# Making the low parts of all projection weight tiles on VectorE instead of GpSimd in a two-layer hybrid decoder trunk

## Chip, cores and metric

The kernel runs on one core of one Trainium2 chip. The metric is the time of one execution in microseconds (us), as the median of several runs. One more execution was taken with the hardware profiler on; all rows in this document come from such profiled executions.

## What is computed

The reference applies two layers to a residual stream x of 1024 tokens by 1024 channels, all in float32:

```python
for l in range(DEPTH):                       # DEPTH = 2
    h = x @ w_in                             # 1024 x 2912
    o_sb = stick_breaking_attention(...)     # 4 heads of 64
    o_mla = mla_mixer(...)                   # 4 heads, softmax attention with low-rank q and kv
    o_rwkv = rwkv7_mixer(...)                # 8 heads, a recurrence over tokens
    mix = concatenate([o_sb, o_mla, o_rwkv], axis=-1) @ w_o
    x = layer_norm(DEEPNORM_ALPHA * x + mix, ln1_g, ln1_b)
    u_act, u_gate = split(x @ ffn_w_up, 2)   # d_ff = 2816
    hid = gelu(causal_depthwise_conv(u_act)) * u_gate
    x = layer_norm(DEEPNORM_ALPHA * x + hid @ ffn_w_down, ln2_g, ln2_b)
```

## The kernel before

Most large products are made of three matrix products. Each float32 operand is split into a high part, a copy in TensorE's reduced type fp32r, and a low part, the operand minus its high part. TensorE then adds high times high, high times low and low times high in PSUM (`mm3`, L203 to L205). The split is one helper, `split`: ScalarE always makes the high part (L198), and the low part is one subtraction (L199) on VectorE, or on GpSimd where the caller names it:

```python
def split(self, hi, lo, src, eng=None):
    self.nc.scalar.copy(hi, src)                                                          # L198
    (eng or self.nc.vector).tensor_tensor(lo, src, hi.bitcast(F32), op=ALU.subtract)      # L199
```

Both inputs of the subtraction and its output lie in SBUF. A weight tile is 128 partitions by 1024 columns. `wload` (L230) loads one from HBM into `raw` and splits it into `whi` and `wlo`; each of the three names has two buffers, so the high part of a tile waits until TensorE has used the tile before last.

A layer runs in four stages. **Phase A** (`phase_a`, about 37 to 540 us of the span in layer 0) makes the input projections and the RWKV work. A loop over four feature tiles `ft` (L1100) makes the k, r and v projections of each by `proj_rw`, prepares them (`rw_prep`, `rw_stage1`), and after each pair starts the inversion of small triangular blocks (`rw_inv`), a generator whose many VectorE steps (L720 to L762) are threaded between other work. After it comes the chain over tokens (`rw_chain`), and beside it the projections for stick-breaking attention (`proj_sb`). **Attention** (about 540 to 735 us) interleaves both attentions; at its end the first two tiles of the output weight are split (L1202). The **output projection** (`oproj`) splits the other six tiles (L949), multiplies, normalizes and transposes. The **FFN** (`ffn`, about 760 to 1550 us) is the rest. Layer 1 follows the same pattern from about 1560 us on.

The splits that name GpSimd are: nine per layer in phase A, for `ft` 1 to 3 (L1101); six per layer in `proj_sb` (L265, L271); two per layer at the end of attention (L1202, tile `w0l`); two per layer in `oproj`, k = 2 and 5 (L949, tile `wol`); two small ones per layer in `mla_prep` (tile `wl`). GpSimd also splits some attention operands (`lo4`, L370), masks the diagonal blocks of stick-breaking attention (L393), multiplies in `rw_stage1` (L640), and serves the chain (L879, L899).

Every engine runs its instructions in one fixed order, which the framework's scheduler writes when the program is built, from the order of the code, the offsets in the table `PRIORITY`, and its own estimate of how long each instruction takes on its engine. An instruction that waits holds everything behind it on that engine. When an instruction goes to another engine, the scheduler writes all the orders anew, so other instructions move too.

Of the kernel before, what the change touches and what calls it, by code (L numbers as in the profile page):

```python
# [17 lines left out]
P = 128  # L18
# [6 lines left out]
SBQ, SBK, SBV = 0, 256, 512  # L25
# [44 lines left out]
class Body:  # L70
# [190 lines left out]
    def proj_sb(self, l, pool, step):  # L261
        nc, W = self.nc, self.a["w_in"][l]
        for j in range(2):
            for base, dst in ((SBQ, self.sqd), (SBK, self.skd)):
                hi, lo = self.wload(W, [(base + j * P, P)], nc.gpsimd)  # L265
                d = self.t(pool, [P, S], "pst", bufs=4)
                self.proj_copy(hi, lo, d)
                nc.sync.dma_start(dst[j], d)
                step(4)
        for j in range(2):  # L270
            hi, lo = self.wload(W, [(SBV + j * P, P)], nc.gpsimd)  # L271
            d = self.t(pool, [P, S], "pst", bufs=4)
            self.proj_copy(hi, lo, d)
            o = self.t(pool, [P, S], "pst", bufs=4)
            for q in range(2):
                pt = self.ps2()
                for i in range(4):
                    ii = 4 * q + i
                    nc.tensor.transpose(pt[:, i * P : i * P + P], d[:, ii * P : ii * P + P], self.ident)
                nc.vector.tensor_copy(o[:, q * 512 : q * 512 + 512], pt)  # L280
            step(4)
            nc.sync.dma_start(self.svd[j], o.rearrange("p (i v) -> p i v", v=P))
# [652 lines left out]
    def oproj(self, l, wr, nxt, side, cm, other, xsrc, co, cx):  # L935
        nc, a = self.nc, self.a
        with cm:
            c = cm
            mp = self.pool(c, "mixp", side=side)
            tp = self.pool(c, "opt", bufs=3, side=side)  # L940
            wh = self.t(mp, [P, KT - 2, D], "woh", F32R)
            wl = self.t(mp, [P, KT - 2, D], "wol", F32R)
            wos = [(self.w0h[:, k], self.w0l[:, k]) for k in range(2)] + [(wh[:, k], wl[:, k]) for k in range(KT - 2)]
            gb = self.bcast(mp, a["ln1_g"][l], "gb")
            bb = self.bcast(mp, a["ln1_b"][l], "bb")
            for k in range(2, KT):
                if k >= len(wr):
                    wr.append(self.wo_load(l, k))
                self.split(*wos[k], wr[k], nc.gpsimd if k % 3 == 2 else None)  # L949
            co.close()  # L950
            self.new_xT(self.pool(cx, "xT", side=other))
            zs = []
            for i in reversed(range(NT)):
                s = slice(i * P, i * P + P)
                mh, ml = nxt
                z = self.t(tp, [P, D], "z")
                nc.sync.dma_start(z, xsrc[s, :])
                zs.append(z)
                ps = self.mm_ps()
                for h in range(2):  # L960
                    hs = slice(h * 512, h * 512 + 512)
                    for k in range(KT):
                        self.mm3(ps[:, hs], mh[:, k, :], ml[:, k, :], wos[k][0][:, hs], wos[k][1][:, hs], k == 0, k == KT - 1)
                    nc.vector.scalar_tensor_tensor(z[:, hs], z[:, hs], ALPHA, ps[:, hs], op0=ALU.mult, op1=ALU.add)
                if i:
                    nxt = self.mix_load(i - 1)
                self.ln_apply(z, z, gb, bb, tp)
                nc.sync.dma_start(self.x1d[s, :], z)
                if i + 1 < NT:
                    self.x_transpose(zs[-2], i + 1, "mt")  # L970
            W = a["ffn_w_up"][l]
            pre = []
            for j in range(2):
                w = self.wload(W, [(j * DFF, P)])
                ps = self.mm_ps()
                self.proj_half(ps, w, 1)
                pre.append((w, ps))
            self.x_transpose(zs[-1], 0, "mt")
        return pre
# [85 lines left out]
    def phase_a(self, l, side, other, lp, co, cc):  # L1065
        nc, a = self.nc, self.a
        c2 = ExitStack()
        ip = self.ip = self.pool(co, "rwi", side=other)
        pp = self.pp_ = self.pool(co, "pst", side=other)
        with ExitStack() as c:  # L1070
            kp = self.pool(c, "mlak", side=other)
            mw = self.pool(c, "mlaw", bufs=2, side=other)
            mc = self.proj_mla(l, pp)
            self.mla_prep(l, mc, kp, mw)
        tpa = self.tpa = self.pool(c2, "rwp", side=other)
        tp = self.pool(c2, "rws", side=other)
        self.q2n, self.q4n = 5, 2
        d = self.proj_rw(l, 12, pp, "pst")
        nc.scalar.activation(d[0:64, :], d[0:64, :], AF.Tanh)
        self.lora = [self.t(tpa, [P, S], f"lora{i}", F32R) for i in range(2)]  # L1080
        self.split(*self.lora, d)
        w2a2 = [self.t(tpa, [P, 512], f"w2a2{i}", F32R) for i in range(2)]
        raw = self.q2(tp)
        nc.sync.dma_start(raw[0:64, :], a["rwkv_w2"][l])
        nc.sync.dma_start(raw[64:128, :], a["rwkv_a2"][l])
        self.split(*w2a2, raw)
        self.Vz = []
        for b in range(1):
            z = self.t(tp, [P, S], f"Vz{b}")
            nc.gpsimd.memset(z, 0.0)  # L1090
            self.Vz.append(z)
        A6 = self.t(ip, [P, 6, NCH, C], "Aa")
        inv = None

        def step(n):
            for _ in range(n):
                if inv is not None:
                    next(inv, None)

        for ft in range(4):  # L1100
            eng = nc.gpsimd if ft else None  # L1101
            k = self.proj_rw(l, 4 + ft, pp, "pst", eng)
            step(6)
            prep = self.rw_prep(ft, k, w2a2, tp)
            r = self.proj_rw(l, ft, pp, "pst", eng)
            step(6)
            v = self.proj_rw(l, 8 + ft, pp, "pst", eng)
            step(99)
            u = (0, 2, 4, 2)[ft]
            for hf in range(2):  # L1110
                self.rw_stage1(ft, hf, [r, k, v], prep, A6[:, u : u + 2], tp)
            if ft % 2:
                inv = self.rw_inv(ft // 2, ip, A6[:, 2 * (ft // 2) : 2 * (ft // 2) + 4])
        c2.close()
        kp = self.pool(cc, "rwk", side=other)
        self.tl = self.pool(cc, "rwl", side=other)
        tp = self.pool(cc, "rwt", side=other)
        g2 = self.t(kp, [P, 512], "g2")
        nc.sync.dma_start(g2, a["rwkv_g2"][l])
        sg = self.sg = self.proj_rw(l, 13, kp, "sg")  # L1120
        nc.scalar.activation(sg, sg, AF.Sigmoid)
        self.rw_chain_state(kp)
        ch = self.rw_chain(0, g2, tp)
        for _ in ch:
            step(3)
        step(99)
        ch = self.rw_chain(1, g2, tp)

        def cstep(n):
            next(ch, None)  # L1130

        self.proj_sb(l, pp, cstep)
        for _ in ch:
            pass

    def run(self):
        nc, a, tc = self.nc, self.a, self.tc
# [27 lines left out]
        for l in range(L):  # L1165
# [15 lines left out]
            with ExitStack() as c:  # L1181
# [17 lines left out]
                nxt = self.mix_load(NT - 1)  # L1199
                wr = [self.wo_load(l, k) for k in range(6)]  # L1200
                for k in range(2):
                    self.split(self.w0h[:, k], self.w0l[:, k], wr[k], nc.gpsimd)  # L1202
            cp.close()
            with ExitStack() as c:
                self.psum(c, ps=(512, 2), mt=(512, 2))
# [42 lines left out]
```

## Time and profile before

| | |
|---|---|
| median of 3 runs | 3118.68 us (3115.67 to 3125.54) |
| the profiled execution's own time | 3115.81 us |
| its span, first to last instruction | 3114.1 us |
| TensorE (PE) busy | 2955.1 us, 95% |
| VectorE (DVE) busy | 1790.4 us, 57% |
| ScalarE (ACT) busy | 1043.3 us, 34% |
| GpSimd (POOL) busy | 328.5 us, 11% |
| mean granted TensorE clock | 0.98 |

PE stands for TensorE's matmuls, PEld for its weight loads, DVE for VectorE, ACT for ScalarE, POOL for GpSimd and SP for the queue that issues the DMAs. In a row, `out<-in` are tile names with their numbers left out, then the shape. In a timeline, `[x <-y]` means that the engine sat idle for x us before the instruction, and y was the event that ended it. The granted clock is given as a share of full speed: 1.00 is 2.4 GHz, 0.50 is 1.2 GHz.

### The profile page before, as it was taken

What the parts mean: (1) busy time and instruction counts of PE and PEld (TensorE: products, weight loads), DVE (VectorE), ACT (ScalarE), POOL (GpSimd) and SP (SyncE); (2) the same over time, 40 slices, a digit from 0 to 9 for tenths busy, and PEclk for the clock granted to TensorE, in tenths of its full rate; (3) what the DMA queues carried; (4) which work ended last, traced back from release to release, by engine and by line L of the source; (5) the groups of instructions that cost most, each with busy time, mean ns of one, the idle gap of its engine ahead of it and who ended that gap; (6) DMA issues with size and microseconds to landing.
All of it is one profiled execution on the core that took longest, in us unless ns stands there. A gap on an engine that the chain in (4) does not pass through costs nothing. (4 is left out here: it accounts for less than half of the span.)

```text
span 3114.1 us, 41891 instructions
## 1 busy us (share of the span) xinstructions
PE 2955.1 (95%) x16572; PEld 2339.9 (75%) x16572; DVE 1790.4 (57%) x2842; ACT 1043.3 (34%) x1801; POOL 328.5 (11%) x346
## 2 busy tenths in 40 slices
PE   8998999888999999999999888999899999999998
PEld 6666777666888888888876667776678888888887
DVE  4569673886644444444645687658865443444436
ACT  5443443763222112221244443447622111212120
POOL 0111231132000000000001121320410000000000
PEclk9998999999999999999999999999999999999999
DMA  4343656413421111111124446563234111111111
GB/s 131 98 143 87 197 176 194 120 52 123 168 68 55 48 41 48 55 48 55 61 81 117 119 114 196 171 203 93 86 126 162 54 41 41 48 55 48 54 48 55
DMA packets 338260, 301.78 MB, mean 97 GB/s; under 512 B 24200, under 2 KB 302992, under 8 KB 338064
## 3 DMA queue, kind: packets, MB, share of 16 engines
q1 hardware_dynamic: 338064, 299.11, 32.4%
q8 instruction: 131, 2.15, 0.3%
q14 instruction: 65, 0.53, 0.1%
HBM read 208.87 MB, written 90.18 MB: 96 GB/s over the span
## 5 line engine op out<-in xcount | busy, mean ns | idle before, releaser
L203 PE MATMUL psmm<-xTh,whi 128*128 128x512 f32 x2144 | 858.3, 400 | 0.0
L204 PE MATMUL psmm<-xTl,whi 128*128 128x512 f32 x2144 | 856.6, 400 | 0.0
L205 PE MATMUL psmm<-xTh,wlo 128*128 128x512 f32 x2144 | 854.2, 398 | 0.0
L198 ACT CAST whi<-raw 128x1024 fp32r<-128x1024 f32 x152 | 159.9, 1052 | 1108.4 <-PE psmm L204 1100.7
L203 PEld LDWEIGHTS psmm<-xTh,whi 128*128 128x128 f32 x2144 | 406.2, 189 | 94.4 <-issue 5.3
L204 PEld LDWEIGHTS psmm<-xTl,whi 128*128 128x128 f32 x2144 | 406.0, 189 | 93.5 <-issue 3.9
L205 PEld LDWEIGHTS psmm<-xTh,wlo 128*128 128x128 f32 x2144 | 405.7, 189 | 93.5 <-issue 4.4
L199 DVE TENSOR_TENSOR wlo<-raw,whi 128x1024 fp32r<-128x1024 f32 x122 | 148.9, 1220 | 430.2 <-ACT whi L198 422.6
L1050 DVE TENSOR_TENSOR y<-y,psps 128x512 f32<-128x512 f32 x288 | 196.4, 687 | 171.7 <-PE psps L205 171.4
L203 PE MATMUL psps<-wdh,hh 128*128 128x512 f32 x672 | 267.0, 397 | 0.0
L204 PE MATMUL psps<-wdl,hh 128*128 128x512 f32 x672 | 263.1, 392 | 0.0
L205 PE MATMUL psps<-wdh,hl 128*128 128x512 f32 x672 | 260.3, 392 | 0.0
L913 POOL TENSOR_TENSOR lrs<-lrs,mhalf 128x1 f32<-128x1 f32 x32 | 29.3, 914 | 1650.4 <-DVE lrs L912 1650.4
L203 PEld LDWEIGHTS psps<-wdh,hh 128*128 128x128 f32 x672 | 126.1, 188 | 36.4 <-ACT hh L198 5.5
L205 PEld LDWEIGHTS psps<-wdh,hl 128*128 128x128 f32 x672 | 126.2, 188 | 27.1
L204 PEld LDWEIGHTS psps<-wdl,hh 128*128 128x128 f32 x672 | 126.3, 188 | 25.8
L1025 DVE TENSOR_TENSOR cv<-cv,psmm 128x1024 f32<-128x1024 f32 x44 | 53.7, 1221 | 142.8 <-PE psmm L205 137.9
L199 DVE TENSOR_TENSOR wdl<-raw,wdh 128x1024 fp32r<-128x1024 f32 x42 | 51.4, 1225 | 89.0 <-ACT wdh L198 89.0
L199 POOL TENSOR_TENSOR wlo<-raw,whi 128x1024 fp32r<-128x1024 f32 x30 | 74.8, 2494 | 194.7 <-ACT whi L198 178.3
L839 PE MATMUL pspa<-RBl,PSl 128*128 128x128 f32 x512 | 71.5, 287 | 17.7 <-ACT QC L842 9.3
L1020 ACT ACTIVATE cv<-cv 128x1024 f32<-128x1024 f32 x44 | 46.7, 1061 | 115.8 <-DVE cv L1019 115.8
L839 PEld LDWEIGHTS pspa<-RBl,PSl 128*128 128x128 f32 x512 | 64.9, 197 | 25.2 <-ACT QC L842 11.2
(444 smaller groups left out, 4696.0 us busy)
## 6 DMA issues: line engine op xcount, KB each, us to landing
raw<-in_ffn_w_up_dram SPq DMA_DIRECT2D x88, 512.0 KB
raw<-in_w_in_dram SPq DMA_DIRECT2D x44, 512.0 KB
raw<-in_ffn_w_down_dram SPq DMA_DIRECT2D x44, 512.0 KB
rbd<-RB SPq DMA_DIRECT2D x64, 256.0 KB
PSl<-psd SPq DMA_DIRECT2D x32, 512.0 KB
RBl<-rbd SPq DMA_DIRECT2D x32, 512.0 KB
psd<-Vz SPq DMA_DIRECT2D x64, 128.0 KB
xxd<-X SPq DMA_DIRECT2D x64, 128.0 KB
```

The lines of the kernel that those rows point to most:

```text
L198: self.nc.scalar.copy(hi, src)
L199: (eng or self.nc.vector).tensor_tensor(lo, src, hi.bitcast(F32), op=ALU.subtract)
L203: mm(out, lh, rh, start=start, stop=False)
L204: mm(out, lh, rl, start=False, stop=False)
L205: mm(out, ll, rh, start=False, stop=stop)
L839: nc.tensor.matmul(pQ[:, f, e, :], PSh[:, f, h, e, :], RBh[:, f, h, e, :], start=True, stop=True)
L913: nc.gpsimd.tensor_tensor(rs, rs, self.mhalf[:, 0:1], op=ALU.pow)
L1020: nc.scalar.activation(cv, cv, AF.Gelu)
L1025: nc.vector.tensor_tensor(cv, cv, pg, op=ALU.mult)
L1050: nc.vector.tensor_tensor(y[:, i, hs], y[:, i, hs], ps, op=ALU.add)
```

## The change

The four places that named GpSimd for the low part of a weight tile of the input or output projection now leave the choice to `split`, which takes VectorE. The small splits of `mla_prep` and the attention operands of `lo4` stay on GpSimd. That moves 19 subtractions of 128x1024 per layer, 38 in all.

```diff
@@ proj_sb
-                hi, lo = self.wload(W, [(base + j * P, P)], nc.gpsimd)
+                hi, lo = self.wload(W, [(base + j * P, P)])
...
-            hi, lo = self.wload(W, [(SBV + j * P, P)], nc.gpsimd)
+            hi, lo = self.wload(W, [(SBV + j * P, P)])
@@ oproj
-                self.split(*wos[k], wr[k], nc.gpsimd if k % 3 == 2 else None)
+                self.split(*wos[k], wr[k])
@@ phase_a
-            eng = nc.gpsimd if ft else None
+            eng = None
@@ run
-                    self.split(self.w0h[:, k], self.w0l[:, k], wr[k], nc.gpsimd)
+                    self.split(self.w0h[:, k], self.w0l[:, k], wr[k])
```

The scheduler's new orders differ in phase A far beyond the 38 rows. Three places on VectorE, all in layer 0; each is a piece of the difference, with `-` for before and `+` for the change.

First, `rw_stage1` for `ft` = 1, around 186 to 196 us of the trace of before. `kk` and `ta` are its inputs, `q_298` and `q_299` the tiles that it hands to TensorE, `wlo_1862` and `wlo_2003` the low parts of the next two weight tiles:

```order
 L614 SCALAR_TENSOR_TENSOR kk_1435<-pst_1375,pv_66_286,kk_1435 128x1024
-L638 SCALAR_TENSOR_TENSOR q_298_1611<-kk_1435,q_296_1604 128x4x63
+L199 TENSOR_TENSOR wlo_1862<-raw_1860,whi_1861 128x1024
 L307 TENSOR_SCALAR shc_1547<-psmm_1548,pv_66_286 128x1
 L308 SCALAR_TENSOR_TENSOR pst_1546<-psmm_1548,pv_66_286,pst_1546 128x511
+L638 SCALAR_TENSOR_TENSOR q_298_1611<-kk_1435,q_296_1604 128x4x63
...
 L646 TENSOR_TENSOR ta_1434<-ta_1434,pst_1375 128x512
 L648 TENSOR_TENSOR q_299_1612<-ta_1434,q_297_1605 128x4x64 x2
-L649 SCALAR_TENSOR_TENSOR ta_1434<-pst_1482,pv_66_286,ta_1434 128x512
+L199 TENSOR_TENSOR wlo_2003<-raw_2001,whi_2002 128x1024
 L305 TENSOR_TENSOR pst_1546<-pst_1546,shc_1547 128x1
```

One low part now stands ahead of the instructions that make `q_298` and `q_299`, the other behind them.

Second, the end of that `rw_stage1` and the start of the inversion, around 219 to 239 us. `q_360` and `q_363` are the low parts of `kk` for `ft` = 2, which TensorE sums over heads (L592); `LA` is the inversion's input:

```order
+L199 TENSOR_TENSOR q_360_1984<-kk_1960,q_359_1983 128x512
+L199 TENSOR_TENSOR q_363_1992<-kk_1960,q_362_1991 128x512
 L684 TENSOR_TENSOR Aa_877<-pspa_1827,maskA_94 128x256
 L685 TENSOR_TENSOR RB_1811<-pspa_1827,maskA_94 128x4x64
 L684 TENSOR_TENSOR Aa_877<-pspy_1828,maskA_94 128x256
 L685 TENSOR_TENSOR RB_1811<-pspy_1828,maskA_94 128x4x64
-L720 STREAM_TRANSPOSE LA_1924<-Aa_877 32x1024 x2
-L305 TENSOR_TENSOR pst_1866<-pst_1866,shc_1867 128x1
-L308 SCALAR_TENSOR_TENSOR pst_1866<-psmm_1896,pv_66_286,pst_1866 128x511
-L720 STREAM_TRANSPOSE LA_1924<-Aa_877 32x1024 x2
+L720 STREAM_TRANSPOSE LA_1924<-Aa_877 32x1024 x4
```

The two low parts moved from behind the four transposes to ahead of them.

Third, the start of the chain, around 384 to 392 us. `QC_3213` is the chain's first operand, `pd` and `T` belong to the second inversion:

```order
 L724 TENSOR_TENSOR pd_3286<-LA_3284,T_3285 128x392
-L725 TENSOR_REDUCE T_3285<-pd_3286 128x2x14
-L724 TENSOR_TENSOR pd_3286<-LA_3284,T_3285 128x450
-L725 TENSOR_REDUCE T_3285<-pd_3286 128x2x15
-L724 TENSOR_TENSOR pd_3286<-LA_3284,T_3285 128x1024
 L840 TENSOR_TENSOR QC_3213<-pspa_3214,arl_3207 64x2x2x64
 L841 TENSOR_TENSOR QC_3213<-pspa_3214,ident_60 64x2x2x64
 L840 TENSOR_TENSOR QC_3213<-pspa_3222,arl_3207 64x2x2x64
 L841 TENSOR_TENSOR QC_3213<-pspa_3222,ident_60 64x2x2x64
```

Four instructions of the inversion that stood ahead of the chain's first operand now stand behind it.

## Rows read from the trace of the kernel before

**Rows 1.** The page: busy time, share of the span and instructions of each engine.

```profile
PE 2955.1 (95%) x16572; PEld 2339.9 (75%) x16572; DVE 1790.4 (57%) x2842; ACT 1043.3 (34%) x1801; POOL 328.5 (11%) x346
```

**Rows 2.** Stretches: from:to, length, busy us (instructions) by engine, granted clock, DMA.

```profile
140.00:160.00 20.00, 17.11 (x122) 12.13 (x121) 13.90 (x28) 8.13 (x19) 4.37 (x4) 1.00 0.38 106
...
140.00:380.00 240.00, 216.32 (x1548) 163.39 (x1546) 180.38 (x315) 107.86 (x209) 43.97 (x47) 0.95 0.48 134
196.00:206.50 10.50, 10.50 (x60) 7.70 (x58) 3.68 (x9) 3.99 (x13) 0.20 (x1) 0.70 0.43 112
...
220.00:300.00 80.00, 66.76 (x479) 50.44 (x477) 74.09 (x115) 32.85 (x59) 16.94 (x11) 0.91 0.34 96
380.00:540.00 160.00, 147.74 (x1333) 117.30 (x1333) 93.11 (x201) 55.83 (x110) 40.49 (x35) 0.99 0.59 186
690.00:745.00 55.00, 43.70 (x279) 31.11 (x279) 41.49 (x61) 27.68 (x66) 19.67 (x16) 0.91 0.40 122
860.00:1520.00 660.00, 660.00 (x2896) 541.99 (x2895) 279.86 (x296) 133.99 (x127) 0.00 (x0) 1.00 0.17 51
```

**Rows 3.** Waits of PE from 110 to 745 us: total us, times, longest.

```profile
PE pspq L671 <- DVE q L648: 8.0, 2, 4.3
PE pspa L336 <- DVE mexp L397: 8.0, 8, 3.0
...
PE pspq L592 <- DVE q L199: 4.8, 1, 4.8
```

**Rows 4.** Groups on L199 by shape: count, busy us, mean ns, idle before them.

```profile
L199 POOL TENSOR_TENSOR wlo<-raw,whi 128x1024 fp32r<-128x1024 f32 x30 | 74.8, 2494 | 194.7 <-ACT whi L198 178.3 <-issue 15.7 <-DMA psd<-T 0.6
...
L199 POOL TENSOR_TENSOR w0l<-raw,w0h 128x1024 fp32r<-128x1024 f32 x4 | 10.7, 2679 | 12.8 <-ACT w0h L198 12.8
L199 POOL TENSOR_TENSOR wol<-pst,woh 128x1024 fp32r<-128x1024 f32 x4 | 10.0, 2508 | 4.6 <-ACT woh L198 4.6
```

```profile
L199 DVE TENSOR_TENSOR wlo<-raw,whi 128x1024 fp32r<-128x1024 f32 x122 | 148.9, 1220 | 430.2 <-ACT whi L198 422.6 <-DMA y<-x1d 7.6
```

**Rows 5.** Timeline of DVE: start, us; two instructions beside GpSimd splits, and the same forms alone.

```profile
116.17 1.89 DVE L305 TENSOR_TENSOR pst<-pst,shc 128x1 f32<-128x1 f32 x1 [3.92 <-ACT pst L303]
...
196.10 0.15 DVE L305 TENSOR_TENSOR pst<-pst,shc 128x1 f32<-128x1 f32 x1
...
723.46 2.86 DVE L396 TENSOR_TENSOR_SCAN pd<-pd,ones 128x255 f32<-128x255 f32 x1
...
728.15 0.69 DVE L396 TENSOR_TENSOR_SCAN LA<-LA,ones 128x255 f32<-128x255 f32 x1
```

**Rows 6.** Timeline around 186 to 196 us, and one row of PE at 144 us.

```profile
143.57 0.30 PE L663 MATMUL pspa<-ident,q 128*128 128x128 f32 x1 [1.67 <-DVE q L639]
...
186.06 2.56 POOL L199 TENSOR_TENSOR wlo<-raw,whi 128x1024 fp32r<-128x1024 f32 x1 [4.54 <-ACT whi L198]
...
186.46 2.44 DVE L638 SCALAR_TENSOR_TENSOR q<-kk,q 128x252 f32<-128x252 f32 x1
...
189.68 0.41 DVE L638 SCALAR_TENSOR_TENSOR q<-kk,q 128x252 f32<-128x252 f32 x1
...
192.50 2.90 DVE L648 TENSOR_TENSOR q<-ta,q 128x256 f32<-128x256 f32 x2
...
195.46 1.11 PE L671 MATMUL pspq<-ident,q 128*128 128x128 f32 x4 [4.29 <-DVE q L648]
```

**Rows 7.** Timeline around the start of the chain, 386 to 392 us.

```profile
386.23 4.11 DVE L724 TENSOR_TENSOR pd<-LA,T 128x1024 f32<-128x1024 f32 x1
...
391.71 0.49 PE L839 MATMUL pspa<-RBl,PSl 128*128 128x128 f32 x2 [3.61 <-ACT QC L842]
```

**Rows 8.** Timeline of the end of attention.

```profile
699.53 3.10 DVE L397 SCALAR_TENSOR_TENSOR mexp<-mexp,T 128x768 f32<-128x768 f32 x1
...
708.12 0.16 DVE L568 RECIPROCAL mst<-mst 128x1 f32<-128x1 f32 x1 [1.65 <-ACT mexp L562]
```

**Rows 9.** Timeline of DVE: a low part of the output projection that VectorE makes already.

```profile
738.08 1.22 DVE L199 TENSOR_TENSOR wlo<-raw,whi 128x1024 fp32r<-128x1024 f32 x1 [4.62 <-ACT whi L198]
```

## The prediction

> **What bounds the kernel now.** I read the shares of busy time first, then the same shares by stretch, then what TensorE waits for, and last the timeline at those waits. TensorE is busy for 95% of the span [rows 1]. In the FFN it has no idle time at all (660.00 of 660 us), and no low part is moved there [rows 2]. So the change can only win or lose in phase A and at the end of attention: TensorE idles 23.7 us in 140 to 380, 12.3 us in 380 to 540 and 11.3 us in 690 to 745, in each layer [rows 2]. There VectorE is the other full engine: 180.38 of 240 us, 74.09 of 80 us in the stretch 220 to 300, and 41.49 of 55 us at the end of attention [rows 2]. The longest waits of TensorE in layer 0 end on VectorE: 4.3 us for `q` of L648, 4.8 us for the low part of `kk`, 3.0 us for `mexp` of L397 [rows 3].
>
> The groups tell why GpSimd matters although it is busy only 11% of the time. One of its low parts takes 2494 ns (30 `wlo`), 2679 ns (4 `w0l`) or 2508 ns (4 `wol`); VectorE makes the same tile in 1220 ns [rows 4]. And while GpSimd makes one, VectorE mostly stands still. An add of one column takes 1.89 us beside such a split, 0.15 us alone; a scan over 255 columns takes 2.86 us, 0.69 us alone [rows 5]. These two are the first and the last of 15 such instructions in layer 0, beside 15 of its 19 splits. Their excess over the same form alone, in us: L305 1.7, 1.7, 2.1, 1.1, 1.7; L638 2.0; L648 2.1, 1.6; L724 2.2, 2.2; L644 2.2; L878 1.5; L397 2.1; L394 2.2; L396 2.2; together 28.6. Such time counts as busy for VectorE, so its true work is less than the shares say.
>
> All stalled forms read two tiles of SBUF, or scale one SBUF tile into SBUF (L394, L878); transposes, reductions and instructions that take one input from PSUM keep their usual time beside a split. The Trainium skill, SBUF — State Buffer, section "Who interferes with whom", gives this rule: a VectorE instruction with two SBUF inputs, or in a two-port mode, and a GpSimd instruction that reads SBUF exclude each other, and the later one waits for the whole of the other. By that rule the other side counts too: VectorE's new low parts can hold GpSimd back.
>
> **The change, part by part, for one layer.** Added on VectorE: 19 x 1.220 = 23.2 us [rows 4]. Removed: the 28.6 us of stalls. Net on VectorE: -5.4 us. ScalarE's part and all DMAs stay as they were. What counts is where TensorE waits.
>
> - *The three splits before 150 us.* Stalls of 1.7, 1.7 and 2.1 go, 3 x 1.22 come: at best -1.9, at worst 0, because VectorE was idle for 3.92 us just before the first of them anyway [rows 5]. I take -0.5, nearer to zero because of that row.
> - *186 to 196 us.* L638 takes 2.44 instead of 0.41, the second L648 some 2.1 too long (2.90 for two), and TensorE idles 4.29 for the result [rows 6]. In the new order one low part stands ahead of these instructions and the other behind. The result comes 2.0 + 2.1 - 1.2 = 2.9 us earlier, and the gap shrinks to some 1.4. After the gap the granted clock is 0.70 over 10.5 us in which TensorE is always busy [rows 2], a mix of the 2.4 and 1.2 GHz levels that costs 0.30 x 10.5 = 3.15. After the gap of 1.67 at 143.57 [rows 6] the stretch shows 1.00 [rows 2]. So between 0 and 3.15 more is given back; half, 1.6, since VectorE sets the pace soon after. Together -4.5.
> - *220 to 300 us.* VectorE is 93% busy here [rows 2]. Stalls of 1.1, 2.2, 1.6 and 2.2 = 7.1 go, 4 x 1.22 = 4.9 come: -2.2. The low part of `kk` moves ahead of four transposes, so the gap of 4.8 [rows 3] can close; but where VectorE is full, a gap that closes opens elsewhere. I take -2.2, with 0 and -7.0 as the ends.
> - *340 to 420 us.* Stalls of 1.7, 2.2 and 1.5 go, four low parts (4.9) come: VectorE gains 0.5. But the 4.11 us product, itself stalled by 2.2, no longer stands ahead of the chain's first operand, for which TensorE waits 3.61 [rows 7]. Between 0 and -3.6; I take the middle, -1.8, because projections may fill or follow that gap either way.
> - *460 and 480 us.* These two splits stall nothing, and VectorE is at 58% in that stretch [rows 2]: 0. The cover is VectorE's free time; without it, +2.4.
> - *End of attention.* Stalls of 2.1, 2.2 and 2.2 = 6.5 go, 4 x 1.22 = 4.9 come, of which one falls where VectorE was idle for 1.65 [rows 8]: between -1.6 and -2.8. The first stall, L397 at 3.10 us [rows 8], is the 3.0 us wait of TensorE [rows 3]. I take -2.0.
>
> Sum: -0.5 - 4.5 - 2.2 - 1.8 + 0 - 2.0 = -11.0 us per layer.
>
> Against it stands a **new wait**. VectorE must now wait for ScalarE's high part at 19 more places, and everything behind waits with it. At the stage after attention, where VectorE already makes such a low part, it waits 4.62 us [rows 9]. Bounds: 0, if every high part is ready, and 19 x 4.62 = 88, if none is. At the place of 186 us the high part is ready in time: GpSimd's split, which waits for it, starts at 186.06, and VectorE reaches the new place right before the 186.46 of L638 [rows 6]. So I take the equal of some half of one such wait, +2.5 us per layer; it also covers what GpSimd's masks lose behind VectorE's low parts.
>
> That leaves -8.5 us per layer, -17 for two. The profiled execution took 3115.8 us, its span and 1.7 us around it, so the forecast is **3099 us**. The median of the runs is 2.9 us above that execution; about 0.3% of it, 9.4 us, is what a measurement here can tell from no change, so below 3109.3 counts as faster and above 3128.0 as slower.
>
> **Rivals.**
>
> - *Only the net counts* (same). If stalls and low parts are equally often on TensorE's path, the win is the net, 5.4 us per layer, by the share of it that TensorE feels, about half: 2 x 2.7 = -5.4, 3110 us. For it: in 220 to 300 VectorE is so full that only its total matters. Against it: the two stalls at 186 to 196 stand right before TensorE's gap, and the new order puts one of the two low parts behind.
> - *The high part comes too late* (slower). VectorE's in-order wait for `whi` takes the place of the stall. Place: `ft` 1 to 3, where `whi` of a tile waits for TensorE to have used the tile before last, while the rest of `rw_stage1` queues behind it on VectorE. Price 4.62 each [rows 9] against a gain of 11.0 without new waits: two exposed waits per layer give a little back, three (13.9) turn the sign, and four give 2 x (18.5 - 11.0) = +15, 3131 us. For it: before the fifteen `wlo` of a layer GpSimd sat idle, waiting, for most of 194.7 us in both layers [rows 4]. Against it: most of that wait was lack of work.
> - *A full engine only gets fuller* (slower). In the full stretch 220 to 300 and at the end of attention the eight added low parts cost 8 x 1.22 = 9.8 us per layer, while the stalled time comes back through other orders: +19.5, 3135 us. The Trainium skill, Perfetto Trace Analysis, section "Optimizing Scalar/DVE Operations", speaks for this: when VectorE is saturated, moving work to GpSimd may make sense, which this change undoes; it adds that the shared port may leave no gain from such a move. The stalls of rows 5 are nearer to the second half.
> - *Both reordered gaps close wholly* (much faster). With the lower ends of all terms, -1.9 - 6.1 - 7.0 - 3.6 - 2.8 = -21.4 per layer and no new wait: 3073 us.
>
> **How the numbers follow.** The forecast gets 0.58, the wholly closed gaps 0.10, only the net 0.22, the late high part 0.06, the fuller engine 0.04. Faster is the first two, 0.68; same 0.22; slower 0.10. The forecast's own range is 3088 to 3109. The range to hold 8 in 10 reaches on to the net rival with some room for an order that fits less well, and down a part of the way to the closed gaps: **3083 to 3118**.
>
> **What would show it.** If right: GpSimd's busy time falls by 38 splits, some 95 us, to about 233 us; VectorE's falls too, by around 10, although it does more; L305 has no instruction over 1 us; the wait for L648 before L671 falls from 4.3 to under 2, and that for L397 from 3.0 to about 1; the granted clock at 196 to 206 rises towards 1.00. The 220 to 300 stretch stays full. Wrong would be: VectorE idle before `wlo` on ScalarE's `whi` in phase A for 3 us and more at several places per layer; or new gaps of TensorE behind `q` or `QC` as long as those that went; or long stalls that remain beside L370 and L640, which GpSimd keeps.

## The result, and the profile after

The changed kernel takes 3079.68 us (median of 4 runs, 3077.35 to 3081.76) against 3118.7 us (3115.67 to 3125.54) of the kernel before: a ratio of 0.9877, 95% interval 0.9859 to 0.9895. That is 39 us less, faster as forecast, but more than twice the forecast 17 us and 3.3 us below the range's low end. The profiled execution took 3081.59 us, 34.2 us less than that of before; the parts below add up to that.

The page after, answering to [rows 1]:

```profile
PE 2958.6 (96%) x16572; PEld 2343.6 (76%) x16572; DVE 1773.6 (58%) x2880; ACT 1042.6 (34%) x1801; POOL 238.3 (8%) x308
```

TensorE's busy time did not fall; it rose by 3.5 us. Its idle time, span less busy time, fell from 3114.1 - 2955.1 = 159.0 to 3079.9 - 2958.6 = 121.3 us. So the whole gain, and a little more, is idle time: 37.7 us. Where it went is seen in the same four stages of layer 0, cut at the first instruction of L638, of L720 on VectorE, of L839, of L557 and of L1048. First before, then after (columns as in [rows 2]):

```profile
142.50:224.80 82.30, 75.31 (x498) 55.29 (x499) 53.91 (x106) 37.37 (x80) 13.46 (x12) 0.96 0.46 130
224.80:381.70 156.90, 139.11 (x1043) 106.94 (x1042) 126.78 (x213) 69.34 (x127) 30.51 (x35) 0.95 0.50 140
381.70:550.90 169.20, 155.52 (x1412) 123.73 (x1414) 100.13 (x216) 63.86 (x124) 41.26 (x37) 0.99 0.60 187
550.90:883.00 332.10, 302.25 (x1833) 235.82 (x1832) 242.46 (x435) 157.60 (x357) 59.54 (x66) 0.95 0.37 115
```

```profile
142.80:220.20 77.40, 75.33 (x513) 55.26 (x514) 53.55 (x113) 41.51 (x86) 5.80 (x9) 1.00 0.51 146
220.20:365.10 144.90, 135.12 (x1021) 103.27 (x1021) 117.24 (x206) 64.50 (x121) 19.11 (x29) 0.95 0.51 144
365.10:538.70 173.60, 160.84 (x1411) 130.16 (x1411) 105.76 (x227) 63.42 (x122) 30.55 (x32) 0.95 0.61 186
538.70:864.30 325.60, 301.53 (x1833) 235.19 (x1834) 239.04 (x438) 158.36 (x359) 48.26 (x62) 0.96 0.38 118
```

The first stage gives 4.9 us, the second 12.0, the chain takes 4.4 back, and the fourth, from the start of attention into the FFN, gives 6.5. With the same cuts, layer 1 has 5.0, 11.5, -3.6 and 0.9. TensorE's idle time in them went from 7.0, 17.8, 13.7 and 29.9 to 2.1, 9.8, 12.8 and 24.1 us. The chain is longer although it idles less: its granted clock fell from 0.99 to 0.95, and its busy time rose by 5.3. After the change it stands at the lower of its two levels, 1.2 GHz, in 371.7 to 378.5, 440.0 to 446.8 and 532.1 to 535.5 us, before only in 383.1 to 386.5; the first of these falls lies in TensorE's wait of 3.8 us for `QC`, which ends at 373.08:

```profile
371.70:378.50 6.80, 5.42 (x22) 4.67 (x24) 5.32 (x11) 3.27 (x5) 0.00 (x0) 0.50 0.19 63
```

The waits of TensorE in layer 0 (110 to 727 us after), answering to [rows 3]:

```profile
PE pspa L839 <- ACT QC L842: 4.9, 2, 3.8
...
PE pspy L591 <- ACT q L198: 3.2, 1, 3.2
...
PE pspa L336 <- DVE mexp L397: 2.6, 5, 0.8
...
PE pspy L592 <- DVE q L199: 1.4, 1, 1.4
...
PE pspq L671 <- DVE q L648: 0.7, 1, 0.7
```

The waits for L648 fell from 8.0 us to 0.7, those for L397 from 8.0 to 2.6. The wait for the split of `kk` did not go: 4.8 before, now 3.2 for its high part and 1.4 for its low part. The chain's first operand is still waited for, 3.8 us. Over the whole kernel TensorE's waits that end on VectorE fell from 106.2 to 58.9 us, and those that end on ScalarE rose from 24.4 to 36.2.

The place around 190 us, answering to [rows 6], and the clock behind it:

```profile
187.02 0.41 DVE L638 SCALAR_TENSOR_TENSOR q<-kk,q 128x252 f32<-128x252 f32 x1
...
190.26 0.76 DVE L648 TENSOR_TENSOR q<-ta,q 128x256 f32<-128x256 f32 x2
190.93 1.22 DVE L199 TENSOR_TENSOR wlo<-raw,whi 128x1024 fp32r<-128x1024 f32 x1
...
191.07 0.66 PE L671 MATMUL pspq<-ident,q 128*128 128x128 f32 x4 [0.68 <-DVE q L648]
```

```profile
191.00:201.50 10.50, 10.43 (x72) 7.40 (x74) 5.34 (x11) 4.42 (x14) 0.20 (x1) 1.00 0.65 174
...
220.00:300.00 80.00, 71.61 (x552) 54.37 (x550) 73.71 (x119) 31.09 (x59) 10.09 (x7) 0.91 0.34 96
```

L638 takes 0.41 in place of 2.44, two L648 take 0.76 in place of 2.90, the gap of 4.29 is 0.68, and the clock after it is 1.00, not 0.70. VectorE in 220 to 300 is as full as before, 73.71 of 80 us, but TensorE now works 71.61 us of it against 66.76 [rows 2].

### The profile page after: what moved, and what is told of

It is laid out like the page before. It is cut to its first block, busy times and chain, and to the rows that moved or that the text cites. A ratio compares the mean times of both kernels' runs of the same rounds, so it can differ in the third digit from the quotient of the medians.

```text
span 3079.9 us, 41861 instructions
## 1 busy us (share of the span) xinstructions
PE 2958.6 (96%) x16572; PEld 2343.6 (76%) x16572; DVE 1773.6 (58%) x2880; ACT 1042.6 (34%) x1801; POOL 238.3 (8%) x308
## 4 chain that ended last, share of the span: by engine, by line
PE 75%; DVE 9%; issue 7%; DMA 3%; ACT 3%; POOL 2%; SPq 0%; POOLq 0%; DVEq 0%; ACTq 0%
PE psmm L204 16%; PE psmm L203 16%; PE psmm L205 16%; PE psps L203 5%; PE psps L205 5%; PE psps L204 5%; PE pspa L839 1%; PE pspi L783 1%; DVE pd L724 1%; PE psmt L214 1%; PE pspa L679 1%; POOL kl L370 1%; DVE Aa L762 0%; DVE T L725 0%; POOL Aa L759 0%
## 5 line engine op out<-in xcount | busy, mean ns | idle before, releaser
L199 DVE TENSOR_TENSOR wlo<-raw,whi 128x1024 fp32r<-128x1024 f32 x152 | 185.6, 1221 | 465.1 <-ACT whi L198 465.0
L199 DVE TENSOR_TENSOR wdl<-raw,wdh 128x1024 fp32r<-128x1024 f32 x42 | 51.5, 1225 | 88.6 <-ACT wdh L198 88.6
L839 PE MATMUL pspa<-RBl,PSl 128*128 128x128 f32 x512 | 74.4, 293 | 13.9 <-ACT QC L842 8.8
L1020 ACT ACTIVATE cv<-cv 128x1024 f32<-128x1024 f32 x44 | 46.7, 1062 | 116.1 <-DVE cv L1019 116.1
L839 PEld LDWEIGHTS pspa<-RBl,PSl 128*128 128x128 f32 x512 | 67.2, 202 | 21.5 <-ACT QC L842 10.7
L204 PE MATMUL psmm<-wol,whi 128*128 128x512 f32 x192 | 77.4, 403 | 2.0 <-DVE wol L199 2.0
```

The source lines that it names most:

```text
L204: mm(out, lh, rl, start=False, stop=False)
L839: nc.tensor.matmul(pQ[:, f, e, :], PSh[:, f, h, e, :], RBh[:, f, h, e, :], start=True, stop=True)
L1020: nc.scalar.activation(cv, cv, AF.Gelu)
```

## The experiments

Each of 15 runs has its ratio to the kernel before, timed on the same chip. "Work" is VectorE's busy time on the page and "idle" TensorE's, worked out as above; these and the clock are of the one profiled execution. The change, profiled a second time as e12, has 121.0 us of idle in place of 121.3.

| run | median us | ratio (95%) | work | PE busy | idle | clock |
|---|---|---|---|---|---|---|
| before | 3118.7 | 1 | 1790.4 | 2955.1 | 159.0 | 0.980 |
| the change | 3079.68 | 0.9877 (0.9859 to 0.9895) | 1773.6 | 2958.6 | 121.3 | 0.980 |
| e1 | 3103.18 | 0.9971 (0.9958 to 0.9983) | 1816.0 | 2948.8 | 144.0 | 0.982 |
| e2 | 3078.65 | 0.9884 (0.9868 to 0.9900) | 1776.2 | 2954.4 | 125.2 | 0.982 |
| e3 | 3064.74 | 0.9842 (0.9825 to 0.9858) | 1735.0 | 2943.9 | 121.6 | 0.985 |
| e4 | 3104.12 | 0.9973 (0.9962 to 0.9983) | 1779.7 | 2956.1 | 145.5 | 0.980 |
| e5 | 3078.86 | 0.9883 (0.9867 to 0.9898) | 1775.3 | 2960.9 | 116.2 | 0.980 |
| e6 | 3081.35 | 0.9892 (0.9877 to 0.9907) | 1783.1 | 2957.7 | 128.3 | 0.980 |
| e7 | 3091.10 | 0.9929 (0.9916 to 0.9943) | 1773.8 | 2957.0 | 131.5 | 0.981 |
| e8 | 3109.10 | 0.9984 (0.9971 to 0.9996) | 1793.7 | 2964.8 | 148.5 | 0.977 |
| e9 | 3073.86 | 0.9862 (0.9844 to 0.9880) | 1812.8 | 2943.2 | 128.3 | 0.984 |
| e10 | 3071.26 | 0.9857 (0.9839 to 0.9874) | 1771.8 | 2952.9 | 114.4 | 0.981 |
| e11 | 3065.69 | 0.9836 (0.9816 to 0.9856) | 1775.5 | 2936.8 | 121.3 | 0.986 |
| e12 | 3080.09 | 0.9885 (0.9867 to 0.9903) | 1773.9 | 2960.5 | 121.0 | 0.980 |
| e13 | 3086.77 | 0.9911 (0.9897 to 0.9925) | 1804.2 | 2950.7 | 135.1 | 0.982 |
| e14 | 3062.32 | 0.9837 (0.9824 to 0.9851) | 1814.4 | 2928.3 | 130.5 | 0.987 |
| e15 | 3050.53 | 0.9799 (0.9785 to 0.9813) | 1789.2 | 2941.6 | 111.3 | 0.985 |

### Is it the stall? (e1, e2, e6)

Three kernels with the same order on every engine. They differ in one operation: behind each of the 38 low parts, GpSimd does something with the raw tile that nobody reads.

```diff
-        (eng or self.nc.vector).tensor_tensor(lo, src, hi.bitcast(F32), op=ALU.subtract)
+        (eng or self.nc.vector).tensor_tensor(lo, src, hi.bitcast(F32), op=ALU.subtract); g and self.nc.gpsimd.tensor_tensor(src, src, hi.bitcast(F32), op=ALU.subtract)
```

For e2 the addition is `self.nc.gpsimd.memset(src, 0.0)`, for e6 `self.nc.gpsimd.tensor_copy(src, src)`; `g` is true at the 38 places.

> The changed kernel, and behind each of the 38 low parts that VectorE now makes, GpSimd makes the same subtraction once more, into the raw tile, which nobody reads (so the outputs stay those of the reference). TensorE waits for none of it; only VectorE can be held back. Theory A (the stalls themselves were on TensorE's path): VectorE's busy time rises by 40 to 60 us of stalls again and the kernel gives back nearly all of its 39 us, 3105 to 3125, or more, since VectorE now has both the low parts and the stalls. Theory B (the gain is the new order and the low part that is done in 1.22 instead of 2.49 us): those stay, so 3080 to 3095.

> The same kernel with the same order on every engine, but GpSimd's 38 extra instructions are memsets of the raw tile: write-only, one input fewer to read, 0.95 us each by the rows of other memsets. Theory A, with the stall coming from GpSimd's reading of SBUF: no stall on VectorE, 3076 to 3086, and the difference to the run before is the price of the stalls alone, 25 to 45 us. If instead any use of GpSimd at these places costs (a later release of the raw tile, its queue): 3090 or more, by 1/2 or more of the difference between the changed kernel and the run before.

> As the run with the second subtraction, with the same order on every engine, but GpSimd's 38 extra instructions copy the raw tile onto itself: one input from SBUF in place of two. If any reading of SBUF by GpSimd holds VectorE's two-input instructions: stalls of VectorE as long as such a copy, 1 to 2.5 us each, 20 us or more in all, and a ratio of 0.992 to 0.998. If it takes two inputs on GpSimd's side: no stalls, and a ratio of 0.987 to 0.989, as with the memsets.

One place in all three timelines, in the order e1, e2, e6:

```profile
128.81 2.77 POOL L199 TENSOR_TENSOR raw<-raw,whi 128x1024 f32<-128x1024 f32 x1 [5.37 <-DVE wlo L199]
129.25 2.35 DVE L305 TENSOR_TENSOR pst<-pst,shc 128x1 f32<-128x1 f32 x1
```

```profile
129.18 0.95 POOL L199 MEMSET raw<- 128x1024 f32 x1 [5.34 <-DVE wlo L199]
129.64 0.15 DVE L305 TENSOR_TENSOR pst<-pst,shc 128x1 f32<-128x1 f32 x1
```

```profile
131.42 1.44 POOL L199 COPY raw<-raw 128x1024 f32<-128x1024 f32 x1 [5.35 <-DVE wlo L199]
131.87 0.99 DVE L305 TENSOR_TENSOR pst<-pst,shc 128x1 f32<-128x1 f32 x1
```

The add of one column ends with GpSimd's instruction: 129.25 + 2.35 = 131.60 beside 128.81 + 2.77 = 131.58, and for the copy 131.87 + 0.99 = 132.86 = 131.42 + 1.44. Beside a memset it takes its 0.15. Counted over the trace, as the excess over the same form alone, the second subtraction stalls VectorE by 44.7 us, the memsets by 2.8, the copies by 9.2.

The memsets cost nothing beside the change; the subtractions cost 24.5 us more than the memsets by the medians, 27 us by the ratios, 18.8 us of idle in the two profiles (the one of e1, 3094.8 us, is the fastest of its runs). These are waits for VectorE: those of TensorE that end on it sum to 83.5 us in e1 and 64.0 in e2. Those that end on a DMA are fewer in e1, 11.0 against 13.9, so a raw tile that comes free later is not the reason. Theory A thus holds for about 27 of the 38 us by the times, and for half of the 37.7 in idle time; for each of the 41.9 us of stalls that e1 has more than e2 it is 0.45 us of idle. e1 came out a little below what theory A expected: VectorE's own subtraction goes ahead, so the stalls fall elsewhere, and there are 44.7 us of them, not the 56.7 of before. The copy's expectation fell: 9 us, not 20 or more. A copy does hold a two-input instruction, but it takes 1.04 us alone, and some of that passes beside instructions that it does not hold: 9.8 of the copies' 46.7 us beside L308, which takes one input from PSUM.

### The low part left out, or late (e3, e5)

e3 is the kernel before with GpSimd's 38 subtractions replaced by memsets of the low tile; e5 is the change with a memset of the low tile behind VectorE's subtraction, for which TensorE waits.

```diff
-        (eng or self.nc.vector).tensor_tensor(lo, src, hi.bitcast(F32), op=ALU.subtract)
+        eng.memset(lo.bitcast(F32), 0.0) if eng is not None and lo.shape[-1] == S else (eng or self.nc.vector).tensor_tensor(lo, src, hi.bitcast(F32), op=ALU.subtract)
```

> The kernel before, but the 38 low parts that GpSimd makes are left out: GpSimd writes zeros into the low tile instead (0.95 us, write-only, not waiting for the high part), so the outputs lack the low parts of these weights. VectorE keeps the work and, nearly, the order of before. Theory A: without the stalls and without VectorE's 46 us of new low parts it is at least as fast as the changed kernel, 3060 to 3082. Theory B (new order): at most the earlier low part is gained, 3100 to 3118.

> The changed kernel with nearly its order, but behind each of the 38 low parts that VectorE now makes GpSimd writes zeros over the low tile (a memset, write-only, 0.95 us), and TensorE waits for that: the low part is there about as late as GpSimd's own was before, without a stall (the outputs lack these low parts). If the earlier low part carries the 10 us that stay gained with the stalls back: 8 to 12 us slower than the changed kernel, a ratio to before of 0.991 to 0.992. If the order of the other instructions carries them, or a low part is hidden behind the two matmuls on the high part that come first: within 4 us of the changed kernel, 0.987 to 0.989.

e5 is level with the change, 0.9883 (e12, on the same chip, 0.9885): a low part that comes sooner is worth nothing that these runs can tell. e3 has nearly the order of before (some 120 of VectorE's 2842 instructions stand elsewhere, in the change some 360), and 37.4 us of idle are gone with 56.7 us of stalls: 0.66 us for each. That is as much as the idle gain of the change, so no order as new as the change's is needed for it. By the ratios e3 is even 11 us faster than the change; in the profiles that is all busy time of TensorE, 14.7 us less, at a granted clock of 0.985 in place of 0.980. In idle time, VectorE's 46 us of low parts cost 125.2 - 121.6 = 3.6 us (e2 beside e3).

### Part by part (e4, e7, e8)

e4 changes only the two lines of `run` and `oproj`, e7 only the line of `phase_a`, e8 only the two of `proj_sb`.

> Of the change only the end of attention and the output projection: the low parts of w0l and of every third wol on VectorE, all 30 of phase A still on GpSimd. The prediction's step for this place: -2.0 us per layer, 3114.7. By the traces of the two kernels, where this stretch ends 5 to 6 us earlier in each layer: -10 to -12, 3107 to 3109. If the gain of this place needs the earlier phases (another order there): within 3 us of the kernel before.

> Of the change only the 18 low parts of ft 1 to 3 (phase A until some 370 us). By the traces of before and after, TensorE's idle time in 142 to 370 falls by 13 us per layer there; if that comes from these low parts alone, and some of it is given back in the chain: -22 to -28, a ratio of 0.991 to 0.993. By the terms of the prediction (-0.5, -4.5, -2.2, half of -1.8, per layer, without the new wait): -16, 0.995.

> Of the change only the 12 low parts of proj_sb, which run beside the second inversion and the chain. By the prediction: half of -1.8 per layer, -2, and nothing for the last two: a ratio of 0.999. If the chain is bounded by TensorE and the projections fill its gaps anyway: 1.000. If these stalls were as dear as those of ft 1 to 3: -10 or more, 0.997 or less.

By the ratios: -8.4, -22.1 and -5.0 us of 3115, together -35.5 against -38.3 of the change. In time the parts add up within their intervals, 3 to 4 us either way for each, and none needs another. In idle time they do not add up: they take off 13.5, 27.5 and 10.5 us, 51.5 together, against 37.7 of the change; why stays open. In e8 the waits of L671 for L648 are still 6.4 us, in e7 they are 0.7, as in the change: the 18 low parts of `ft` 1 to 3 carry the place that [rows 3] lead with. e4 and e7 are worth more than their terms in the prediction (-4 and -16); for e8 (-2) the interval, -9 to -1 us, leaves it open.

### What VectorE's time costs (e9, e13, e14)

e9 makes the 38 subtractions twice on VectorE. e13 makes the products of L648 four times over, which TensorE waits for. e14 makes the same products three times into `bv`, ahead of L653, which overwrites them.

```diff
-            nc.vector.tensor_tensor(BK[:, :, 1 - e, e, :], pv4(av)[:, :, e, :], iG4[:, :, e, :], op=ALU.mult)
+            [nc.vector.tensor_tensor(BK[:, :, 1 - e, e, :], pv4(av)[:, :, e, :], iG4[:, :, e, :], op=ALU.mult) for _ in range(4)]
```

> The changed kernel, and VectorE makes each of the 38 subtractions a second time, into the raw tile, which nobody reads: 38 x 1.22 = 46 us more work on VectorE that the scheduler knows of. By the difference of the memset run and the run without these low parts (13 us for 49 us of VectorE time, 0.27 us each): +12, a ratio to before of 0.991 to 0.993. If a microsecond of VectorE's work costs as much as a microsecond of stall (49 us for 56, 0.88 each): +41, a ratio of 1.000 or more. If VectorE has so much free time that it hides it: 0.988.

> The changed kernel, but each of the 32 products of L648 is made four times over (the same values into the same tile), so that TensorE's next transposes wait for 2.5 us more of VectorE at each of 16 places: 96 x 0.417 = 40 us of VectorE work, as long as the stalls were, and as the doubled low parts. If VectorE's time costs by the place, and not by the amount: TensorE's idle time grows by 0.6 to 0.9 of it, +24 to +36 beside the change, a ratio of 0.996 to 1.000. If any added VectorE work is as cheap as the doubled low parts were (7 us more of TensorE idle for 46 us): +4 to +7, 0.990.

> The control: the changed kernel and the same 96 products in the same stage, but two instructions later, into a tile that L653 overwrites and nothing on TensorE waits for (40 us of VectorE work). By the place: 0.1 to 0.2 of it, +4 to +8, 0.989 to 0.991. By the amount: as the run before.

46 us more of VectorE's work made the kernel 7 us faster than the change on the same chip (e12), not slower: idle rose by 7.3, but TensorE's busy time fell by 17.3 for the same 16572 matmuls, at a mean clock of 0.984 in place of 0.980. e14 is the same with 40 us: 9.2 more idle than the change, 30.3 less busy, clock 0.987. So the ratios expected of e9 and e14 missed; of the two of e13, the cheap one, 0.990, lies in its interval, but its idle grew by 13.8 us, which neither named. The pair e13 and e14 does differ by 24 us, and with e13 TensorE waits for VectorE in this stage again:

```profile
PE pspa L663 <- DVE q L639: 5.2, 3, 2.7
...
PE pspy L663 <- DVE q L639: 2.9, 1, 2.9
...
PE pspq L671 <- DVE q L648: 2.5, 1, 2.5
```

In e14 it waits 1.9 us for L639 and 2.8 for L648, so what e13 adds lies at L639, not at the products themselves. And between the two profiles only 4.6 us are idle; 22.4 are busy time, and the orders of the two differ in many rows. What stands is that work which the scheduler plans for costs 0.08 to 0.35 us of idle for each (3.6 for 46, 7.3 for 46, 9.2 for 40, and 13.8 for 40 in e13), in every case less than the stall's 0.45 (e1 beside e2) to 0.66 (e3). Whether the place alone sets that price stays open.

### Versions faster than both (e10, e11, e12, e15)

What still stalls VectorE after the change is GpSimd's own work beside L370 (8.6 us) and L640 (6.1 us). e12 is the change again, as a base.

```diff
-SPLIT_STICK = (0, 4)
+SPLIT_STICK = (0, 0)
...
-            nc.gpsimd.tensor_tensor(AR[:, 1, :, s_, :], pv4(pr_)[:, :, e, :], G4[:, :, e, :], op=ALU.mult)
+            nc.vector.tensor_tensor(AR[:, 1, :, s_, :], pv4(pr_)[:, :, e, :], G4[:, :, e, :], op=ALU.mult)
...
-        nc.gpsimd.tensor_tensor(mo, mo, bvl, op=ALU.add)
+        nc.vector.tensor_tensor(mo, mo, bvl, op=ALU.add)
```

e10 has the first edit, e11 the first two, e15 all three and `mla_prep`'s two splits on VectorE.

> A candidate for a faster version: the changed kernel, and the low parts of the attention operands (lo4) on VectorE as well, whole in place of four pieces. Takes away 8.6 us of stalls beside L370 and adds some 9.8 us of VectorE work (4 tiles of 128x1024 and 4 of 64x1024 by 1.22). By the two prices, 0.88 for a stall and 0.27 for planned work: -7.6 + 2.6 = -5, a ratio of 0.986. By one price for both: +1, 0.988.

> As the candidate before, and the 32 products of L640 on VectorE too: 6.1 us of stalls go, 32 x 0.42 = 13 us of work come. By the two prices: -5.4 + 3.6 = -1.8 beside the candidate before, so -7 beside the change, 0.9855. By one price: +7 more, 0.990 to 0.991.

> The changed kernel again, on the chip of the three runs above, as the base of their comparison: its ratio of 0.9877 again, 0.986 to 0.990.

> The candidate with lo4 and L640 on VectorE, and also the sum of L899 (32 x 0.42 = 13 us of work, 1.0 us of stalls) and the two small splits of mla_prep (no stall that touches TensorE). By the prices of stall and work: +1 to +2 beside that candidate, 0.984 to 0.985. If the order comes out better or worse, as between the other candidates: up to 8 us either way.

The change again gives 0.9885. e10 is 8.8 us faster than it, with 6.6 less idle, e11 14.4. e15 is the fastest, 0.9799, 64 us below the kernel before on its chip, with 111.3 us of idle; no instruction of VectorE stands out over its form beside GpSimd any more. For e10 the prices were right within the noise: 0.986 lies in its interval, and -5 us were expected where 6.6 of idle went. That e11 came out faster is luck: the prices are of idle time, and its idle, 121.3 us, is no less than that of e12; its gain is busy time, 23.7 us less at a mean clock of 0.986. e15 was to be 1 to 2 us slower than e11 and is some 11 faster by the ratios. Busy time moves by up to 24 us between these orders, which the prices leave out.

## Why the prediction was wrong in size

**What was right.** The sign, the cause, and the first two terms: -0.5 and -4.5 were forecast until 196 us; the first stage is 4.9 us shorter in layer 0 and what lies ahead of it 0.3 longer. The stalls went and the clock rose to 1.00 as written; the gap fell to 0.68, below the 1.4 of the text. GpSimd's busy time fell to 238.3 (forecast 233), VectorE's by 16.8 (forecast 10), no L305 takes over 1 us (longest 0.63). Of the signs of being wrong, two came all the same: waits for `whi` of 3 us and more (below), and stalls beside L370 and L640 that remain.

**Where the missing part lies.** As the mean of the two layers, a layer became 17.1 us shorter, and 8.5 were forecast. Of the 8.6 between them, 3.7 lie in the terms of 220 to 420 us, 2.5 in the new wait and 3.9 in the end of attention; the attention ahead of it, which had no term, gave 2.2 back, and 0.7 came outside the stages.

**220 to 420 us: -2.2 and -1.8, measured -7.6.** This is the second and third stage together, -12.0 + 4.4 (layer 1: -11.5 + 3.6), and holds the term of 460 and 480 us, forecast 0, too. [rows 3] say that L671 waits for L648 8.0 us in **two** waits. The prediction priced the one of 4.3 and left the other in the stretch that it called too full for a gap to close. It lies here, in the trace of before:

```profile
260.24 2.34 POOL L199 TENSOR_TENSOR wlo<-raw,whi 128x1024 fp32r<-128x1024 f32 x1 [8.73 <-ACT whi L198]
...
260.87 2.00 DVE L648 TENSOR_TENSOR q<-ta,q 128x256 f32<-128x256 f32 x1
...
262.79 1.91 DVE L724 TENSOR_TENSOR pd<-LA,T 128x1024 f32<-128x1024 f32 x1
264.62 0.40 DVE L648 TENSOR_TENSOR q<-ta,q 128x256 f32<-128x256 f32 x1
...
265.08 1.12 PE L671 MATMUL pspq<-ident,q 128*128 128x128 f32 x4 [3.72 <-DVE q L648]
```

The first L648 stalls for 1.6 us, a product of the inversion (L724) follows, and TensorE waits 3.72 us for the second L648; that wait is gone after. It needs no new order: e3 has the same L724 between its two L648, without the stall, and the two waits for L648 sum to 1.7 us in place of 8.0:

```profile
PE pspq L671 <- DVE q L648: 1.7, 2, 1.2
```

The two gaps for which the text allowed a gain, `kk` and `QC`, stayed (4.6 and 3.8 us). So the fourth rival, with 3073 us nearest to the result, is not what happened either: its gaps did not close.

**Netting stall against work.** Each term took the added 1.22 us of a low part off the stall that went, one for one. This is the step that failed most widely. e3, without the stalls and without these low parts, has 37.4 us less idle than the kernel before; the change, which makes all of them on VectorE, 46.4 us, has 37.7 less. By e3 a stall costs 0.66 us of idle for each microsecond, by e1 beside e2 0.45; these low parts on VectorE cost 0.08 (e2 beside e3) to 0.16 (e9). A likely reason, which no run shows by itself, is that a stall strikes whatever instruction is next, and the order has no room for it, while a low part is put into the order. With these prices the sum would be -26 to -37 for 56.7 us of stalls and +4 to +7 for 46.4 us of low parts, -18 to -34, where the trace has -37.7 of idle: nearer than the forecast's -14, but still short.

**The new wait: +2.5 per layer, measured nothing where it was put.** At its moved low parts in phase A of layer 0 VectorE does wait for `whi`, three times as long as the text named for a sign that it was wrong, 3 us and more:

```profile
117.54 1.23 DVE L199 TENSOR_TENSOR wlo<-raw,whi 128x1024 fp32r<-128x1024 f32 x1 [3.33 <-ACT whi L198]
...
129.86 1.23 DVE L199 TENSOR_TENSOR wlo<-raw,whi 128x1024 fp32r<-128x1024 f32 x1 [3.08 <-ACT whi L198]
...
469.82 1.23 DVE L199 TENSOR_TENSOR wlo<-raw,whi 128x1024 fp32r<-128x1024 f32 x1 [10.81 <-ACT whi L198]
```

None makes TensorE wait. The first two take the place of idle time that VectorE had there anyway (3.92 us at the first [rows 5], 3.68 at the second), and at the last TensorE is in the middle of a projection. e5 says the same of a late low part. The rival of the late high part is thereby out.

One wait for a high part did grow, at the output projection, for the tile of [rows 9], whose low part VectorE made before too. The first row is of before, the others are of after:

```profile
738.10 0.50 PE L203 MATMUL psmm<-w0h,whi 128*128 128x512 f32 x1 [1.30 <-ACT whi L198]
```

```profile
719.81 1.04 ACT L198 CAST whi<-raw 128x1024 fp32r<-128x1024 f32 x1 [2.65 <-DMA raw<-mixd]
...
720.91 0.79 PE L203 MATMUL psmm<-w0h,whi 128*128 128x512 f32 x1 [3.16 <-ACT whi L198]
```

ScalarE now sits idle until the DMA lands that brings the mixers' output (`mixd`), and TensorE waits 3.16 us, in layer 1 3.08, where it waited 1.30. Both layers together have 6.2 us of it in place of 2.6; e4, which changes this place alone, has 6.3, e7 still 2.6. So 1.8 us per layer of what the end of attention gained were lost again here, and the prediction had no term for it.

**End of attention: -2.0, measured -7.2 and -4.6.** The fourth stage as a whole is 6.5 us shorter in layer 0 and 0.9 in layer 1, but that mixes two things. From the first split of `w0h` on, where the moved low parts begin, it is 7.2 and 4.6 us shorter (before, then after, layer 0 above layer 1):

```profile
698.00:883.00 185.00, 171.88 (x822) 134.89 (x821) 115.48 (x166) 54.08 (x88) 25.47 (x22) 0.96 0.42 141
...
2238.10:2419.80 181.70, 170.66 (x821) 133.93 (x820) 115.81 (x165) 54.21 (x88) 24.31 (x22) 0.97 0.44 143
```

```profile
686.50:864.30 177.80, 169.78 (x821) 132.66 (x820) 112.44 (x169) 53.99 (x88) 14.27 (x18) 0.98 0.44 146
...
2208.60:2385.70 177.10, 169.69 (x820) 132.55 (x820) 112.35 (x170) 54.18 (x88) 14.23 (x18) 0.98 0.45 147
```

The attention ahead of it, where nothing was moved, became longer, from 147.1 to 147.8 us and in layer 1 from 147.1 to 150.8, of which 2.5 are busy time at a clock of 0.93 in place of 0.95. The mean at the place itself is -5.9. One wait that went there is no stall: TensorE waited 1.8 us in each layer for GpSimd's low part `wol` itself, for which the prediction had no term; after the change it waits 1.0 for VectorE's.

```profile
PE psmm L204 <- POOL wol L199: 1.8, 1, 1.8
```

**The clock.** The text gave it -1.6 per layer, at one gap. That gain came (72 matmuls in the 10.5 us behind the gap, 60 before), but the chain lost more: over the kernel TensorE's busy time rose by 3.5 us. The forecast's idle part was thus some -14 against -37.7 measured.

**The chances.** Faster had 0.68 and came. The rival by which only the net counts (3110 us) is out by the time, and by e3 beside the change. The rival of the fuller engine (3135 us) is out by e9, where 46 us more work on VectorE left the kernel no slower. The range was too narrow below: its low end allowed for a part of the closed gaps, but not for the netting being wrong in every term at once.

## What to carry to other kernels

When GpSimd works beside a full VectorE, add up how much longer VectorE's instructions take than the same form alone, and look for TensorE's waits behind them: here 0.45 to 0.66 us of idle time went with each microsecond of that sum. Do not net it one for one against work that the scheduler can place. Read every wait of a group, not the longest alone. Between orders that differ, expect TensorE's busy time to move through the granted clock, here by up to 36 us, and look at idle and busy time apart.

## What the runs showed of the hardware

The stall goes by operation. Beside GpSimd's subtraction or its copy, when that began first, an instruction of VectorE with two inputs in SBUF lasts until GpSimd's ends (e1, e6); beside a memset it does not (e2). But L394, a scale of one SBUF tile, is held by a memset too. In e2:

```profile
694.01 1.45 DVE L394 TENSOR_SCALAR LA<-mexp 128x639 f32<-128x639 f32 x1
694.17 0.94 POOL L199 MEMSET raw<- 128x1024 f32 x1
```

The same form takes 0.48 us elsewhere. It also works the other way: after the change GpSimd's copy of 8 columns, mostly 0.20 us, takes 1.73 us beside a product of 2.00 us:

```profile
253.53 2.00 DVE L724 TENSOR_TENSOR pd<-LA,T 128x1024 f32<-128x1024 f32 x1
253.87 1.73 POOL L632 COPY Gc<-q 128x8 f32<-128x8 f32 x1 [15.86 <-ACT q L630]
```

The Trainium skill, SBUF — State Buffer, section "Who interferes with whom", states all three: two SBUF inputs contend only with a GpSimd instruction that reads, a tensor_scalar in a two-port mode with any, and whoever is first holds the other for its whole length. The rows agree on the first, with 2.35, 0.15 and 0.99 us for L305, and L394, 1.45 us, is held by a memset as the second says, though no view shows in which mode it runs. On who is first, GpSimd's copy agrees: L724 began 0.34 us ahead of it. L394 does not tell, since it began beside GpSimd's mask (L393), which ran until 694.22.

Not expected was how far the granted clock follows the order. For the same 16572 matmuls TensorE's busy time lies between 2928.3 us (e14, mean clock 0.987) and 2964.8 (e8, 0.977). These are one profile each, and executions of one kernel differ too: the clock of the kernel before lies between 0.976 and 0.982, that of e14 between 0.984 and 0.987. The spread of 36 us is as large as the change itself, and why one order gets more of the full clock than another was not tried.
